# Low parts on one engine, regrouped block sums and a third weight buffer in a two-layer encoder kernel

## The chip, the cores and the metric

The kernel runs on one core of a Trainium2 chip. The metric is the device time of one execution in microseconds (us). A core has five engines that run their own instruction streams: TensorE (PE in the profile; its weight loads are PEld), VectorE (DVE), ScalarE (ACT), GpSimd (POOL) and SyncE (SP), which here only issues DMAs. An engine runs its instructions in the order in which they stand, and waits on semaphores for others. 128x512 means 128 partitions by 512 elements.

## The reference

Two encoder layers on 256 tokens of width 2048, in float32. Each layer has token-mixer heads and four heads that attend into 256 memory tokens, an output projection, and a squared-ReLU MLP of width 8192. The change sits almost wholly in the MLP:

```
n = rms_norm(h, mlp_norm[i])
h = h + jnp.square(jax.nn.relu(n @ w_up[i])) @ w_down[i]
...
return rms_norm(h, final_norm)
```

## The kernel before

**Three products for one.** TensorE multiplies a rounded float32 type. To keep precision, each operand is split into a high part (ACT copies it to the rounded type) and a low part (source minus high part, on DVE); each block product is then three matmuls, high by high, high by low and low by high. `split` writes both parts. So all weights, 398 MB read from memory, pass through ACT and one subtraction on the way to TensorE.

**The steps of the MLP.** After six leading up chunks, each layer runs 58 equal steps (`STEPS`, from the table `RUNS`). A step `n` has four grains, in this order: the first part of a down product, two halves of one up chunk (`ps_u`, 24 matmuls of 256 columns each), and the second part of the down product. The down products use Strassen's scheme in Winograd's form: a block of 2 by 2 sub-blocks of activations (`c`, from which `squared` makes seven left factors, split into `a_s`) times a block of 2 by 2 sub-blocks of weights takes seven products, `p1` to `p7`, of three 512-column matmuls each, instead of eight. The four sub-blocks of weights arrive as one tile `b` (`load` of `down_grains`); `pre` adds three or four sums of them, the tile `t`; `prep_first` splits `b` into `bh`, `bl`, and `prep_second` splits `t` into `th`, `tl`. The products accumulate in seven PSUM banks over a run of 4, 6 or 8 steps. At the end of a run `taken` adds each bank to a result column of `h` or to a sum `z` in SBUF, and after the last run of a column half `folded` adds the `z` to `h` in eight operations, spread over the following grains.

**Buffers.** The tiles `bh`, `bl`, `th`, `tl` have one buffer each: the split for step n+1 can begin only when step n's matmuls on that tile are over. The up halves `uh`, `ul` have two. `b`, `T` (holds `t`) and `U` (raw up chunks) have two each. How many grains ahead a load, `pre` and a split are placed is a triple per grain (`ahead`, `SOON`, `SOONER`).

**Who makes the low parts.** Inside the 58 steps the low part of the first up half is made on DVE, that of the second half on POOL (`half_of_side(..., engine=nc.gpsimd if hf and not lead else None)`); all other low parts are on DVE. POOL also issues one DMA a step that adds `b[:, 1]` into `b[:, 3]` in place (L1074); it waits for the sum at L1073, which still needs the old `b[:, 3]`, and `prep_first` waits for its landing.

After the steps the rest of the down weights runs as plain products (`plain_grains`), and in layer 1 `finish` normalises and stores the two token halves.

The order on each engine is set when the program is built, by the order in which these functions run and by a list scheduler on top.

Of the kernel before, what the change touches and what calls it, by code (L numbers as in the profile page):

```python
# [157 lines left out]
def encoder_kernel(ctx: ExitStack, tc: tile.TileContext, t: dict, out: bass.AP):  # L158
# [62 lines left out]
    soon = {}  # L221
    for c, src in ((FIRST_CHUNKS, t["w_km0"][3]), (FIRST_CHUNKS + 1, t["w_vm0"][0])):
        soon[c] = at.work.tile([P, CH], F32, tag="l4", name="raw_l4")
        nc.sync.dma_start(soon[c], src)
    ident = const.tile([P, P], F32, name="ident")
    ones = const.tile([P, P], F32, name="ones")
    nc.gpsimd.memset(ones, 1.0)
# [246 lines left out]
            plan.append(Work("M", blocks[b][0][c], acts, c * 4, begins, last, start, blocks[b][1]))  # L474


    def split(dst_hi, dst_lo, src, engine=None):

        first = nc.scalar.activation(dst_hi, src, AF.Copy)  # L479
        engine = engine or nc.vector  # L480
        return first, engine.tensor_tensor(dst_lo, src, dst_hi.bitcast(F32), op=ALU.subtract)  # L481

    def rstd_of(ss, n, name):

# [361 lines left out]
    def o_done(layer, nb):  # L846
# [16 lines left out]
        def scaled(b):  # L863

            if b < 2:
                box["room", b] = at.side.tile([P, 2, 1024], F32, tag="b", bufs=2, name="h_t")
# [71 lines left out]

    FIRST = ("p3", 6, 0), ("p1", 0, 1), ("p2", 2, 2), ("p5", 3, 3)
    SECOND = ("p7", 4, 0), ("p6", 5, 1), ("p4", 1, 2)

    def half_of_side(raw, hf, place=0, engine=None):
        s = slice(place // 4, place // 4 + HALF)
        tiles = tuple(at.side.tile([P, HALF + 64], F32R, tag=n, bufs=2, name=n)[:, s] for n in ("uh", "ul"))
        box.setdefault("splits", []).append(split(*tiles, raw[:, hf * HALF : (hf + 1) * HALF], engine))
        return tiles

    def loaded(src, tag):  # L950
        raw = at.side.tile([P, CH], F32, tag=tag, bufs=2, name=f"raw_{tag}")
        nc.sync.dma_start(raw, src)
        return raw

    def up_grains(layer, m):
        own = {}
        lead = m < LEAD

        def load():
            own["raw"] = loaded(t[f"w_up{layer}"][m], "U")  # L960

        def prep(hf):

            with tc.issue_after(box["summed"].ins) if m in (1, 2) else nullcontext():
                prepared(hf)

        def prepared(hf):
            half = 2 * m + hf
            if lead and (half in (2, 4) or half > 4 and half % 3 == 2):

                if half < 5:
                    room = at.side.tile([P, 2, HALF], F32R, tag="b", bufs=2, name="u_b")
                    own[hf] = room[:, 0], room[:, 1]
                else:
                    s = slice(U_AT // 4, U_AT // 4 + HALF)
                    own[hf] = tuple(at.mlp.tile([P, 3 * 512], F32R, tag=x, name=f"u_{x}")[:, s] for x in ("th", "tl"))
# [36 lines left out]
    def squared(layer, m, ps):  # L1013
# [12 lines left out]
            a = at.mlp.tile([P, 2, 4, P], F32R, tag="a", bufs=6, name="a_p")  # L1026
            split(a[:, 0], a[:, 1], c[:, :4])
        else:
            for d, x, y, op in ((4, 2, 0, ALU.subtract), (5, 1, 0, ALU.add), (6, 5, 2, ALU.subtract),
                                (7, 3, 6, ALU.subtract)):  # L1030
                box["made"] = nc.vector.tensor_tensor(c[:, d, :], c[:, x, :], c[:, y, :], op=op)  # L1031
# [22 lines left out]
    def down_grains(layer, n, begins, ends, sooner):  # L1054
# [12 lines left out]

        def pre():

            b, s = own["b"], at.side.tile([P, 3, 512], F32, tag="T", bufs=2, name="t")  # L1070

            with tc.issue_after(box["made"].ins) if n == 2 else nullcontext():
                box["t3"] = nc.vector.tensor_tensor(s[:, 0, :], b[:, 3, :], b[:, 0, :], op=ALU.add)  # L1073
            nc.gpsimd.dma_start(b[:, 3, :], b[:, 1, :], accum_op=ALU.add)  # L1074
            nc.vector.tensor_tensor(s[:, 1, :], s[:, 0, :], b[:, 1, :], op=ALU.add)
            nc.vector.tensor_tensor(s[:, 2, :], s[:, 1, :], b[:, 2, :], op=ALU.add)  # L1076
            own["t"] = s

        def prep_first():
            own["first"] = tuple(at.mlp.tile([P, CH], F32R, tag=x, name=x) for x in ("bh", "bl"))  # L1080
            b = own["b"].rearrange("p a b -> p (a b)")
            if sooner:

                with tc.issue_after(box["t3"].ins):
# [2 lines left out]
                split(*own["first"], b)  # L1087

        def prep_second():
            own["second"] = tuple(at.mlp.tile([P, 3 * 512], F32R, tag=x, name=x) for x in ("th", "tl"))  # L1090
            split(*own["second"], own["t"].rearrange("p a b -> p (a b)"))

        def run(which, products):
# [18 lines left out]
        def after_second():  # L1112
# [1 line left out]
            if ends:  # L1114
                box["z_set"].add(q)
            if ends and j == STEPPED[q] - 1:
                folded(q, 0.5 if n == len(STEPS) - 1 else 2)

        return [Grain(lambda: run("first", FIRST), lambda: after(FIRST), load, behind(pre), behind(prep_first, 4 if n else 1),
                      SOONER if sooner else SOON),  # L1120
                Grain(lambda: run("second", SECOND), after_second, None, None, behind(prep_second), SOONER)]

    def open_strassen(layer):

        closed(*[x for x in reversed(list(pools)) if x in ("ps_acc", "ps_att")])
        at.sums = opened("ps_sums", space=bass.MemoryType.PSUM)
        first = [x[0] for x in FIRST]
        second = ["up"] + [x[0] for x in SECOND]
# [34 lines left out]
    def folded(q, gap):  # L1163
# [8 lines left out]
            return lambda: add_scaled(columns_of(i, q, b), z, factor[:, i : i + 1])  # L1172

        for n, fn in enumerate((out(1, 0, z1, inv), add(z6, z6, z1, ALU.subtract), add(z7, z6, z7, ALU.subtract),
                                add(z6, z6, z5), out(1, 1, z6, inv), out(0, 0, z7, inv), add(z7, z7, z5),
                                out(0, 1, z7, ninv))):
            later(1 + int(gap * n), lambda fn=fn: past(fn, box["splits"][-2]))

# [124 lines left out]
    def finish(w, i, bank, begin, end):  # L1303
# [35 lines left out]
        nc.scalar.activation(p[1], p[1], AF.Copy, scale=r)  # L1339
        nc.vector.tensor_scalar(p[2], p[2], r, None, op0=ALU.mult)  # L1340
# [304 lines left out]
```

## Time and profile before

| | us |
|---|---|
| median of 3 runs (2029.22 to 2033.86) | 2031.28 |
| span of the profiled execution, first to last instruction | 2032.0 |
| PE busy in it | 1999.7 |
| DVE busy in it | 1793.5 |
| layer 0, steps 2 to 57 (from 482.26 to 1060.81 us) | 578.55 |
| layer 1, the same steps (from 1405.33 to 1983.80 us) | 578.47 |

The profile gives the span of the profiled execution and no time around it; the median of the unprofiled runs is 0.7 us under the span. Busy time of PE is modelled, since matmuls are pipelined: a new matmul starts while the one before it drains. So a duration of a single matmul (277 ns for 256 columns) is not its price; the distance from one start to the next is. The same holds on a smaller scale on DVE and ACT, where an instruction's record begins a little before that of the one ahead of it ends.

### The profile page before, as it was taken

To read this page: it belongs to the slowest core of one execution; us is meant where nothing else is said; L and a number is where in the kernel's file an instruction comes from. 1 tells how busy PE (TensorE), PEld (TensorE's weight loads), DVE (VectorE), ACT (ScalarE), POOL (GpSimd) and SP (SyncE) were. 2 spreads that over 40 slices of the span, in tenths; PEclk is the share of its full clock that TensorE was granted. 3 is DMA by queue.
4 is the path that set the end of the run, shared out by engine and by line. 5 is a ranking of instruction groups with operands and counts; after the bars stand their busy time and mean duration, and the time that the engine had idled before them with its cause. 6 is when DMAs were issued, how large, how long until landed. Compare 5 with 4: busy or idle time off the path is not lost.

```text
span 2032.0 us, 32807 instructions
## 1 busy us (share of the span) xinstructions
PE 1999.7 (98%) x12920; PEld 1813.0 (89%) x12920; DVE 1793.5 (88%) x2024; ACT 1270.8 (63%) x1735; POOL 541.2 (27%) x261
## 2 busy tenths in 40 slices
PE   9999999999999999999999999999999999999998
PEld 8999999899999898888888888899999898898987
DVE  6777767589999999999999769779999999999997
ACT  6655545567676666666656566567666666666654
POOL 0000000003333544444430010003444544444440
PEclk9999999999999999999999999999999999999999
DMA  7856665667777777677766765557777676776763
GB/s 286 312 199 200 209 203 196 248 188 228 236 230 232 217 230 224 219 231 224 222 203 225 244 213 182 203 171 234 234 232 232 224 239 213 220 240 215 232 197 135
DMA packets 105708, 448.02 MB, mean 220 GB/s; under 512 B 10961, under 2 KB 38609, under 8 KB 58065
## 3 DMA queue, kind: packets, MB, share of 16 engines
q1 hardware_dynamic: 88560, 414.99, 58.7%
q0 software_dynamic: 16704, 30.42, 8.7%
q8 instruction: 101, 1.65, 0.3%
q10 hardware_dynamic: 288, 0.52, 0.1%
q14 instruction: 55, 0.44, 0.1%
HBM read 398.17 MB, written 4.19 MB: 198 GB/s over the span
## 4 chain that ended last, share of the span: by engine, by line
PE 77%; DVE 12%; issue 4%; DMA 3%; POOL 3%; ACT 1%; DVEq 0%; SPq 0%; POOLq 0%; ACTq 0%
PE ps_u L384 24%; PE ps_s L384 10%; PE ps_m L361 8%; PE ps_m L365 8%; PE ps_m L364 8%; PE p L1105 6%; PE p L1102 6%; PE p L1104 6%; POOL ul L481 3%; DVE ul L481 2%; DMA b<-in_w_pair 2%; DVE tl L481 2%; DVE t L1076 2%; DVE c L1031 1%; DVE t L1073 1%
## 5 line engine op out<-in xcount | busy, mean ns | idle before, releaser
L384 PE MATMUL ps_u<-hT,uh 128*128 128x256 f32 x3812 | 668.3, 277 | 0.0
L384 PEld LDWEIGHTS ps_u<-hT,uh 128*128 128x128 f32 x3812 | 581.9, 189 | 5.5
L384 PE MATMUL ps_u<-hT,ul 128*128 128x256 f32 x1960 | 545.7, 278 | 20.6 <-POOL ul L481 17.8
L481 POOL TENSOR_TENSOR ul<-raw_U,uh 128x1024 fp32r<-128x1024 f32 x116 | 417.3, 3597 | 261.1 <-ACT uh L479 261.1
L479 ACT ACTIVATE uh<-raw_U 128x1024 fp32r<-128x1024 f32 x262 | 276.2, 1058 | 231.2 <-PE ps_u L384 221.2
L384 PEld LDWEIGHTS ps_u<-hT,ul 128*128 128x128 f32 x1960 | 369.4, 188 | 24.7 <-POOL ul L481 19.8
L481 DVE TENSOR_TENSOR lo<-raw,hi 128x1024 fp32r<-128x1024 f32 (+1 forms) x215 | 254.7, 1191 | 98.4 <-ACT hi L479 97.3
L479 ACT ACTIVATE hi<-raw 128x1024 fp32r<-128x1024 f32 (+1 forms) x215 | 221.2, 1036 | 162.6 <-PE ps_m L365 84.7
L479 ACT ACTIVATE bh<-b 128x2048 fp32r<-128x2048 f32 x116 | 222.1, 1915 | 78.8 <-PE p L1105 76.3
L481 DVE TENSOR_TENSOR bl<-b,bh 128x2048 fp32r<-128x2048 f32 x116 | 265.0, 2284 | 1.0 <-ACT bh L479 1.0
L481 DVE TENSOR_TENSOR tl<-t,th 128x1536 fp32r<-128x1536 f32 x116 | 238.2, 2054 | 18.0 <-ACT th L479 17.8
L1074 POOL DMA_DIRECT2D b<-b x116 | 102.1, 880 | 525.1 <-DVE t L1073 361.4
L481 DVE TENSOR_TENSOR ul<-raw_U,uh 128x1024 fp32r<-128x1024 f32 x146 | 215.4, 1476 | 6.6 <-ACT uh L479 6.6
L479 ACT ACTIVATE th<-t 128x1536 fp32r<-128x1536 f32 x116 | 172.8, 1489 | 32.4 <-PE p L1105 30.5
L1104 PE MATMUL p<-bl,a_s 128*128 128x512 f32 x464 | 180.8, 390 | 1.6 <-DVE bl L481 1.6
L1105 PE MATMUL p<-bh,a_s 128*128 128x512 f32 x464 | 181.3, 391 | 0.0
L1102 PE MATMUL p<-bh,a_s 128*128 128x512 f32 x464 | 180.6, 389 | 0.0
L384 PE MATMUL ps_s<-nT,hi 128*128 128x256 f32 x896 | 154.7, 276 | 0.0
L1031 DVE TENSOR_TENSOR c<-c 128x128 f32<-128x128 f32 x240 | 144.6, 622 | 5.2 <-ACT c L1021 3.4
L1102 PE MATMUL p<-th,a_s 128*128 128x512 f32 x348 | 136.1, 391 | 0.0
L1104 PE MATMUL p<-tl,a_s 128*128 128x512 f32 x348 | 135.9, 391 | 0.0
L384 PEld LDWEIGHTS ps_s<-nT,hi 128*128 128x128 f32 x896 | 135.5, 188 | 0.2
(295 smaller groups left out, 3772.3 us busy)
## 6 DMA issues: line engine op xcount, KB each, us to landing
raw_U<-in_w_up SPq DMA_DIRECT2D x128, 1024.0 KB, 4.8
b<-in_w_pair SPq DMA_DIRECT2D x116, 1024.0 KB, 4.8
raw<-in_w_o SPq DMA_DIRECT2D x32, 1024.0 KB, 5.0
b<-b POOLq DMA_DIRECT2D x116, 256.0 KB, 3.3
raw<-in_w_b SPq DMA_DIRECT2D x21, 1024.0 KB, 5.1
raw<-in_w_av SPq DMA_DIRECT2D x12, 1024.0 KB, 4.9
raw<-in_w_aq SPq DMA_DIRECT2D x12, 1024.0 KB, 4.8
raw<-in_w_ak SPq DMA_DIRECT2D x12, 1024.0 KB, 4.7
```

The costliest lines, as they stand in the source:

```text
L361: first = nc.tensor.matmul(ps, ah, hi[:, s], start=st, stop=False)
L364: nc.tensor.matmul(ps, ah, lo[:, s], start=False, stop=False)
L365: final = nc.tensor.matmul(ps, al, hi[:, s], start=False, stop=sp)
L384: ins = nc.tensor.matmul(ps, x, acts[:, k, part], start=k == n == 0, stop=k == KT - 1 and n == 2)
L479: first = nc.scalar.activation(dst_hi, src, AF.Copy)
L481: return first, engine.tensor_tensor(dst_lo, src, dst_hi.bitcast(F32), op=ALU.subtract)
L1031: box["made"] = nc.vector.tensor_tensor(c[:, d, :], c[:, x, :], c[:, y, :], op=op)
L1074: nc.gpsimd.dma_start(b[:, 3, :], b[:, 1, :], accum_op=ALU.add)
L1076: nc.vector.tensor_tensor(s[:, 2, :], s[:, 1, :], b[:, 2, :], op=ALU.add)
L1102: ins = nc.tensor.matmul(ps, a[:, 0, ai, :], hi[:, s], start=begins, stop=False)
L1104: nc.tensor.matmul(ps, a[:, 0, ai, :], lo[:, s], start=False, stop=False)
L1105: nc.tensor.matmul(ps, a[:, 1, ai, :], hi[:, s], start=False, stop=ends)
```

## The change

All low parts go to DVE: `split` and `half_of_side` lose their engine argument. The four sums of `squared` become three operations, the second of which makes two blocks at once (with a sign turned, so that `folded` subtracts where it added). The block `b[:, 3] + b[:, 1]` is no longer made in place: ACT copies `b[:, 3]` into a fourth block of `t`, and the DMA adds `b[:, 1]` there, beside the three sums. So `bh`, `bl` shrink from 2048 to 1536 columns and `th`, `tl` grow from 1536 to 2048, and the product `p5` moves from a step's first part to its second. `b` gets a third buffer; the descriptor scratch of DMAs issued by POOL shrinks to 4096 bytes, which makes room for it; the loads of the down blocks are placed 12 grains ahead instead of 8. The fold after the first column half is spread at three grains instead of two. Outside the MLP, one early weight chunk is loaded in two DMAs, and `finish` stores each token half in three DMAs instead of four.

```diff
-        nc.sync.dma_start(soon[c], src)
+        for s in [slice(0, HALF), slice(HALF, CH)] if c == FIRST_CHUNKS else [slice(0, CH)]:
+            nc.sync.dma_start(soon[c][:, s], src[:, s])
...
-    def split(dst_hi, dst_lo, src, engine=None):
+    def split(dst_hi, dst_lo, src):
         first = nc.scalar.activation(dst_hi, src, AF.Copy)
-        engine = engine or nc.vector
-        return first, engine.tensor_tensor(dst_lo, src, dst_hi.bitcast(F32), op=ALU.subtract)
+        return first, nc.vector.tensor_tensor(dst_lo, src, dst_hi.bitcast(F32), op=ALU.subtract)
...
-    FIRST = ("p3", 6, 0), ("p1", 0, 1), ("p2", 2, 2), ("p5", 3, 3)
-    SECOND = ("p7", 4, 0), ("p6", 5, 1), ("p4", 1, 2)
+    FIRST = ("p3", 6, 0), ("p1", 0, 1), ("p2", 2, 2)
+    SECOND = ("p7", 4, 0), ("p6", 5, 1), ("p4", 1, 2), ("p5", 3, 3)
+    BANKS = ("p3", "p1", "p2", "p5"), ("up", "p7", "p6", "p4")
...
-                own[hf] = half_of_side(own["raw"], hf, engine=nc.gpsimd if hf and not lead else None)
+                own[hf] = half_of_side(own["raw"], hf)
...
-            for d, x, y, op in ((4, 2, 0, ALU.subtract), (5, 1, 0, ALU.add), (6, 5, 2, ALU.subtract),
-                                (7, 3, 6, ALU.subtract)):
-                box["made"] = nc.vector.tensor_tensor(c[:, d, :], c[:, x, :], c[:, y, :], op=op)
+            nc.vector.tensor_tensor(c[:, 4, :], c[:, 0, :], c[:, 2, :], op=ALU.subtract)
+            nc.vector.tensor_tensor(c[:, 5:7, :], c[:, 0:5:4, :], c[:, 1, None, :].to_broadcast([P, 2, P]), op=ALU.add)
+            box["made"] = nc.vector.tensor_tensor(c[:, 7, :], c[:, 3, :], c[:, 6, :], op=ALU.subtract)
...
-            own["b"] = at.side.tile([P, 4, 512], F32, tag="b", bufs=2, name="b")
+            own["b"] = at.side.tile([P, 4, 512], F32, tag="b", bufs=3, name="b")
...
-            b, s = own["b"], at.side.tile([P, 3, 512], F32, tag="T", bufs=2, name="t")
+            b, s = own["b"], at.side.tile([P, 4, 512], F32, tag="T", bufs=2, name="t")
+            nc.scalar.activation(s[:, 3, :], b[:, 3, :], AF.Copy)
+            nc.gpsimd.dma_start(s[:, 3, :], b[:, 1, :], accum_op=ALU.add)
...
-            nc.gpsimd.dma_start(b[:, 3, :], b[:, 1, :], accum_op=ALU.add)
...
-                folded(q, 0.5 if n == len(STEPS) - 1 else 2)
+                folded(q, 0.5 if n == len(STEPS) - 1 else 3)
...
-                      SOONER if sooner else SOON),
+                      (12, 8, 4) if sooner else (12, 5, 4)),
...
-        p = [h[:, i, a:b] for a, b in ((0, 256), (256, 768), (768, x))]
+        p = [h[:, i, a:b] for a, b in ((0, 512), (512, x))]
...
-        for eng, a, b in ((nc.sync, 0, 256), (nc.sync, x, D), (nc.scalar, 256, 768), (nc.sync, 768, x)):
+        for eng, a, b in ((nc.sync, x, D), (nc.scalar, 0, 512), (nc.sync, 512, x)):
...
-    nc = _bacc.Bacc("TRN2", target_bir_lowering=False, num_devices=1)
+    nc = _bacc.Bacc("TRN2", target_bir_lowering=False, num_devices=1, dynamic_dma_scratch_size=4096)
```

**DVE in an ordinary step.** Below is what stands on DVE in one step of layer 0 before (a step in which a pair of up chunks is done, so that the split `a_s` and three of the four sums `c` are in it; the fourth stands one step earlier); `t<-b` and `t<-t,b` are the sums of `pre`.

```order
L1073 TENSOR_TENSOR t<-b 128x512
L1075 TENSOR_TENSOR t<-t,b 128x512
L481 TENSOR_TENSOR bl<-b,bh 128x2048
L1076 TENSOR_TENSOR t<-t,b 128x512
L481 TENSOR_TENSOR ul<-raw_U,uh 128x1024
L1031 TENSOR_TENSOR c<-c 128x128 x3
L481 TENSOR_TENSOR tl<-t,th 128x1536
L481 TENSOR_TENSOR a_s<-c,a_s 128x896
```

The same place of the changed program, where all lines behind the first edit stand one further down:

```order
L481 TENSOR_TENSOR bl<-b,bh 128x1536
L1076 TENSOR_TENSOR t<-b 128x512
L481 TENSOR_TENSOR ul<-raw_U,uh 128x1024
L1077 TENSOR_TENSOR t<-t,b 128x512
L481 TENSOR_TENSOR ul<-raw_U,uh 128x1024
L1078 TENSOR_TENSOR t<-t,b 128x512
L1030 TENSOR_TENSOR c<-c 128x128
L1031 TENSOR_TENSOR c<-c 128x256
L1032 TENSOR_TENSOR c<-c 128x128
L481 TENSOR_TENSOR tl<-t,th 128x2048
L481 TENSOR_TENSOR a_s<-c,a_s 128x896
```

DVE has a second `ul` per step, three operations for the sums `c`, and the 512 columns of the added block have moved from `bl` to `tl`. POOL's stream in the MLP, which held an `ul` and a DMA per step, now holds 58 DMAs in a row per layer.

**ACT in an ordinary step.** Before, a step without a pair (`u` is the small copy of an up chunk's first columns, with its buffer's number in the name):

```order
L479 ACTIVATE th<-t 128x1536
L479 ACTIVATE bh<-b 128x2048
L984 ACTIVATE u_5817<-raw_U 128x128
L479 ACTIVATE uh<-raw_U 128x1024 x2
L1020 ACTIVATE c<-ps_u 128x256
L1021 ACTIVATE c<-c 128x256
```

After, the same:

```order
L480 ACTIVATE th<-t 128x2048
L480 ACTIVATE bh<-b 128x1536
L985 ACTIVATE u_6025<-raw_U 128x128
L1072 ACTIVATE t<-b 128x512
L480 ACTIVATE uh<-raw_U 128x1024 x2
L1021 ACTIVATE c<-ps_u 128x256
L1022 ACTIVATE c<-c 128x256
```

The copy that the DMA adds to stands between the split of `b` and those of the up halves, one step ahead of the `th` that reads its result.

**DVE behind the end of the run that `folded` follows** (layer 0, just behind step 51; the `z` are the sums in SBUF, `first` is the tile that holds `h`). Before:

```order
L481 TENSOR_TENSOR tl<-t,th 128x1536
L1169 TENSOR_TENSOR z_4605<-z_4605 128x512
L1031 TENSOR_TENSOR c<-c 128x128
L1073 TENSOR_TENSOR t<-b 128x512
L481 TENSOR_TENSOR bl<-b,bh 128x2048
L481 TENSOR_TENSOR ul<-raw_U,uh 128x1024
```

After:

```order
L481 TENSOR_TENSOR tl<-t,th 128x2048
L1170 TENSOR_TENSOR z_4606<-z_4606 128x512
L1031 TENSOR_TENSOR c<-c 128x256
L481 TENSOR_TENSOR ul<-raw_U,uh 128x1024
L1076 TENSOR_TENSOR t<-b 128x512
L481 TENSOR_TENSOR bl<-b,bh 128x1536
```

Here an `ul` now stands ahead of the `bl` that the next step's first product waits for; before it stood behind it.

More of the change, by code (lines that the diff above doesn't have):

```diff
@@ L865, in scaled @@
             if b < 2:
-                box["room", b] = at.side.tile([P, 2, 1024], F32, tag="b", bufs=2, name="h_t")
+                box["room", b] = at.side.tile([P, 2, 1024], F32, tag="b", bufs=3, name="h_t")
                 y = box["room", b][:, 0]
@@ L932, in add_o, with half_of_side @@
                 plan[-1].behind = plan[-2].behind = plan[-1].last_block = True
-    FIRST = ("p3", 6, 0), ("p1", 0, 1), ("p2", 2, 2), ("p5", 3, 3)
-    SECOND = ("p7", 4, 0), ("p6", 5, 1), ("p4", 1, 2)
-    def half_of_side(raw, hf, place=0, engine=None):
+    FIRST = ("p3", 6, 0), ("p1", 0, 1), ("p2", 2, 2)
+    SECOND = ("p7", 4, 0), ("p6", 5, 1), ("p4", 1, 2), ("p5", 3, 3)
+    BANKS = ("p3", "p1", "p2", "p5"), ("up", "p7", "p6", "p4")
+    def half_of_side(raw, hf, place=0):
         s = slice(place // 4, place // 4 + HALF)
         tiles = tuple(at.side.tile([P, HALF + 64], F32R, tag=n, bufs=2, name=n)[:, s] for n in ("uh", "ul"))
-        box.setdefault("splits", []).append(split(*tiles, raw[:, hf * HALF : (hf + 1) * HALF], engine))
+        box.setdefault("splits", []).append(split(*tiles, raw[:, hf * HALF : (hf + 1) * HALF]))
         return tiles
     def loaded(src, tag):
-        raw = at.side.tile([P, CH], F32, tag=tag, bufs=2, name=f"raw_{tag}")
+        raw = at.side.tile([P, CH], F32, tag=tag, bufs=2 + (tag == "b"), name=f"raw_{tag}")
         nc.sync.dma_start(raw, src)
@@ L971, in prepared @@
                 if half < 5:
-                    room = at.side.tile([P, 2, HALF], F32R, tag="b", bufs=2, name="u_b")
+                    room = at.side.tile([P, 2, HALF], F32R, tag="b", bufs=3, name="u_b")
                     own[hf] = room[:, 0], room[:, 1]
@@ L975, in prepared @@
                     s = slice(U_AT // 4, U_AT // 4 + HALF)
-                    own[hf] = tuple(at.mlp.tile([P, 3 * 512], F32R, tag=x, name=f"u_{x}")[:, s] for x in ("th", "tl"))
+                    own[hf] = tuple(at.mlp.tile([P, CH], F32R, tag=x, name=f"u_{x}")[:, s] for x in ("th", "tl"))
                 box["splits"].append(split(*own[hf], own["raw"][:, hf * HALF : (hf + 1) * HALF]))
             else:
-                own[hf] = half_of_side(own["raw"], hf, engine=nc.gpsimd if hf and not lead else None)
+                own[hf] = half_of_side(own["raw"], hf)
             if not lead and hf == 0:
@@ L1079, in prep_first @@
         def prep_first():
-            own["first"] = tuple(at.mlp.tile([P, CH], F32R, tag=x, name=x) for x in ("bh", "bl"))
-            b = own["b"].rearrange("p a b -> p (a b)")
+            own["first"] = tuple(at.mlp.tile([P, 3 * 512], F32R, tag=x, name=x) for x in ("bh", "bl"))
+            b = own["b"][:, :3].rearrange("p a b -> p (a b)")
             if sooner:
@@ L1089, in prep_second @@
         def prep_second():
-            own["second"] = tuple(at.mlp.tile([P, 3 * 512], F32R, tag=x, name=x) for x in ("th", "tl"))
+            own["second"] = tuple(at.mlp.tile([P, CH], F32R, tag=x, name=x) for x in ("th", "tl"))
             split(*own["second"], own["t"].rearrange("p a b -> p (a b)"))
@@ L1126, in open_strassen @@
         at.sums = opened("ps_sums", space=bass.MemoryType.PSUM)
-        first = [x[0] for x in FIRST]
-        second = ["up"] + [x[0] for x in SECOND]
+        first, second = BANKS
         box["ps"], box["unused"] = {}, set()
```

5 lines of the change are left out of this document (2 added, 3 removed).

## The prediction

> **What bounds the kernel now.** I read the page's busy times first, then who waited for whom on PE, then the chain of waits in order of time, then the time line of the places where PE waited.
>
> ```profile
> span 2032.0 us, 32807 instructions
> ...
> PE 1999.7 (98%) x12920; PEld 1813.0 (89%) x12920; DVE 1793.5 (88%) x2024; ACT 1270.8 (63%) x1735; POOL 541.2 (27%) x261
> ```
>
> PE is busy for 98% of the span, so no change that leaves the matmuls alone can win more than about 32 us. This one leaves them alone: the same seven products of three matmuls, one of them moved. The question is only which part of PE's lost time goes. PE's own waits:
>
> ```profile
> PE ps_u L384 <- POOL ul L481: 17.8, 10, 3.3
> PE ps_u L384 <- DVE ul L481: 2.6, 5, 0.9
> PE p L1104 <- DVE bl L481: 1.6, 2, 1.0
> ```
>
> (us in total, times, longest.) Nearly all of it is for the low part of the second up half, made on POOL: ten waits, 17.8 us. What such a wait costs in the end is read from the chain, where each step's 48 up matmuls are a piece, when they ran without a break:
>
> ```profile
> 482.26 5.45 PE ps_u L384 x48
> 492.49 5.45 PE ps_u L384 x48
> ...
> 1060.81 5.45 PE ps_u L384 x48
> ...
> 1405.33 5.45 PE ps_u L384 x48
> ...
> 1983.80 5.45 PE ps_u L384 x48
> ```
>
> A step without a wait takes 492.49 - 482.26 = 10.23 us. From step 2 to step 57 are 55 steps: 55 x 10.23 = 562.6 us, against 578.55 in layer 0 and 578.47 in layer 1. So the steps lose 16.0 + 15.9 = **31.9 us**, more than the waits name, since weight loads and the pipe behind a wait start anew. Now why POOL is late:
>
> ```profile
> 1009.59 2.28 DVE L481 TENSOR_TENSOR bl<-b,bh 128x2048 fp32r<-128x2048 f32 x1
> 1009.97 0.88 POOL L1074 DMA_DIRECT2D b<-b  x1 [6.78 <-DVE t L1073]
> ...
> 1011.36 9.53 POOL L481 TENSOR_TENSOR ul<-raw_U,uh 128x1024 fp32r<-128x1024 f32 x1 [0.51 <-ACT uh L479]
> ...
> 1011.79 1.22 DVE L481 TENSOR_TENSOR ul<-raw_U,uh 128x1024 fp32r<-128x1024 f32 x1
> ```
>
> The POOL subtraction takes 9.53 us while DVE works beside it without a gap. Over the layers and in layer 0's steps (ns, min/median/max):
>
> ```profile
> L481 DVE TENSOR_TENSOR ul<-raw_U,uh x146: 1186/1220/3455, 369.8 to 2008.9; 128x1024 fp32r<-128x1024 f32 x146
> L481 POOL TENSOR_TENSOR ul<-raw_U,uh x116: 2394/3284/9540, 458.4 to 1980.1; 128x1024 fp32r<-128x1024 f32 x116
> L481 DVE TENSOR_TENSOR tl<-t,th x57: 1740/1752/3455, 459.7 to 1051.0; 128x1536 fp32r<-128x1536 f32 x57
> L1031 DVE TENSOR_TENSOR c<-c x112: 276/286/2504, 457.9 to 1031.5; 128x128 f32<-128x128 f32 x112
> L481 DVE TENSOR_TENSOR a_s<-c,a_s x28: 1079/1085/1090, 464.4 to 1035.1; 128x896 fp32r<-128x896 f32 x28
> L481 DVE TENSOR_TENSOR bl<-b,bh x57: 2277/2284/2292, 466.1 to 1052.7; 128x2048 fp32r<-128x2048 f32 x57
> L1073 DVE TENSOR_TENSOR t<-b x56: 674/687/2742, 463.1 to 1043.1; 128x512 f32<-128x512 f32 x56
> L1075 DVE TENSOR_TENSOR t<-t,b x56: 677/687/694, 463.8 to 1045.9; 128x512 f32<-128x512 f32 x56
> L1074 POOL DMA_DIRECT2D b<-b x56: 880/880/887, 464.1 to 1044.1; - x56
> L1076 DVE TENSOR_TENSOR t<-t,b x56: 676/685/2910, 465.4 to 1047.6; 128x512 f32<-128x512 f32 x56
> ```
>
> The two engines shut each other out. POOL's subtraction is 2.4 us at best and four times that at worst; DVE operations have a firm floor (their medians) and, in some executions, two microseconds more: those are the ones that met a running POOL subtraction. `bl` and L1075, which stand where POOL is issuing its DMA or idle, are never late, and the DMA is 880 to 887 ns although `bl` runs beside it. So the subtraction costs both engines, the DMA issue neither.
>
> **The change, part by part.**
>
> *Low parts to DVE.* It removes 116 POOL subtractions and adds 116 of 1.22 us on DVE. The cover for this is that DVE's stretched operations fall back to their medians. A step on DVE then, by medians: two `ul` 2 x 1.22; `tl`, now 2048 columns, 2.28 (row `bl`); `bl`, now 1536, 1.75 (row `tl`); three sums `t` 3 x 0.69; half a pair's `a_s` 0.54; half a pair's sums `c`. These become three operations, two of 0.29 and one of 256 columns, which no row here shows; it lies between 0.29 (128) and 0.69 (512), and I take 0.42, a third of the way by columns. Half a pair: 0.50. Sum 9.57 us of a step of 10.23. The records overlap, though:
>
> ```profile
> 1050.44 0.68 DVE L481 TENSOR_TENSOR a_p<-c,a_p 128x512 fp32r<-128x512 f32 x1
> 1051.05 1.75 DVE L481 TENSOR_TENSOR tl<-t,th 128x1536 fp32r<-128x1536 f32 x1
> 1052.71 2.28 DVE L481 TENSOR_TENSOR bl<-b,bh 128x2048 fp32r<-128x2048 f32 x1
> 1054.92 1.21 DVE L481 TENSOR_TENSOR ul<-raw_U,uh 128x1024 fp32r<-128x1024 f32 x1
> ```
>
> From start to start these take 0.61, 1.66 and 2.21 us, 0.08 less than their durations. With nine operations a step that makes 9.57 - 0.72 = **8.85 us of 10.23**: 1.4 us free in a step.
>
> [...]
>
> *Does each part come in time?* A step's clock: 69 matmuls; the 48 of up take 5.45 us, so the 21 others 0.228 each. Let F, the first part (now 9 matmuls), start at 0: F ends at 2.05, the up halves at 4.8 and 7.5, S, the second part (now 12), at 10.23. ACT's prices:
>
> ```profile
> L479 ACT ACTIVATE uh<-raw_U 128x1024 fp32r<-128x1024 f32 x115 | 121.3, 1059 | 105.3 <-PE ps_u L384 105.2
> L479 ACT ACTIVATE bh<-b 128x2048 fp32r<-128x2048 f32 x57 | 109.2, 1915 | 38.3 <-PE p L1105 38.3
> L479 ACT ACTIVATE th<-t 128x1536 fp32r<-128x1536 f32 x57 | 84.9, 1489 | 15.7 <-PE p L1105 15.7
> ```
>
> `th` (1.9, as `bh` was) can start at 0, when the S before is over; DVE's `tl` runs 1.9 to 4.2, and S needs it at 7.5: 3.3 us to spare. `bh` 2.05 to 3.6, `bl` to 5.9, with an `a_s` between to 6.9; the next F needs it at 10.23: 3.3 to spare. `ul` of the first half ends near 8, needed at 12.3; of the second (ready at 8.6) near 9.7, needed at 15. At a run's end `taken` adds six operations on 128x512, about 0.7 each by row L1075: 4 us within a step, against 1.4 free in it and 1.4 in the next. Those of the three F products fall where DVE waits for `th` anyway; the rest makes the next `tl` some 1 us late, `bl` about the same. The spare 3.3 us covers it, and all banks are read long before the next step writes them. Behind the run that `folded` follows, eight more operations (5.5 us) come over six steps, 0.9 a step of the 1.4. There the order has an `ul` ahead of `bl`; worked through row by row, `bl` ends some 0.1 us after F asks for it. I put 0.5 us per layer there, **1.0 us** in all. ACT was busy for 63% of the span; the rows above lie on a line (0.43 us per 512 columns), by which the new 512-column copy is some 0.6 us, 6% of a step.
>
> *Three-operation sums.* They are in the sum above; DVE's free time hides them, and without them a step would have 0.1 us less.
>
> *The added block.* `bl` no longer waits for the DMA; `th` now does. ACT copies at about 4.6, the DMA is issued at 5.2, and `th` wants it at 10.23, on pain of a stall from 13.5 on (7.5 of the next step, less 1.9 and 2.3). Landings of DMAs on `b`, the loads included:
>
> ```profile
> DMA to landing us min/median/max: 3.3/4.7/7.9
> ```
>
> 5.2 + 7.9 = 13.1 is in time. Behind `th` on ACT stand `bh` and the `uh` of that step, which share the 3.3 us. Cost 0. Its other end: nothing is won either, since PE never waited for this DMA.
>
> *Third buffer, loads 12 grains ahead, 4 KB of scratch.* PE waits for no load in the list above, so the earlier loads win 0 on PE by themselves; they keep ACT's copy from standing in front of a late load. The smaller scratch could hold up an issue: at the low end 0, at the high end each issue waits until the DMA before has landed. That one was issued 10.23 us earlier and landed after 7.9 at most, so both ends are 0.
>
> *The ends.* The last stores: the final half's ScalarE part loses 256 columns and DVE's gains them; the last DMA leaves some 0.1 us earlier and is 256 columns larger. I take 0, with 0.5 us on either side. The split early load touches nothing that PE waits for: 0.
>
> **The sum**, against the profiled execution: 2032.0 - 31.9 + 1.0 = 2001.1 us. The median of the runs is 0.7 us below the profiled span, so I predict **2000.4 us**, 1.5% less.
>
> **The rivals.**
>
> *DVE becomes the bound in bursts.* If durations count in full, a step has 0.65 us free and not 1.4, and a run's end and the fold (24 + 24 + 8 operations of 0.7, 39 us a layer) use it up: 58 x 9.57 + 39 = 594 us against 58 x 10.23 = 593, plus 0.6 to 1.4 us in each of some steps in which DVE stands waiting for `th`. That is 1 to 7 us per layer: 2002 to 2015 us; I say 2009. The starts above speak against it, the tight `bl` behind the fold for it. [...]
>
> *DVE does not get faster, and the change costs.* If the stretched operations owe their two microseconds to something else than POOL's subtractions (POOL's DMA, or loads into the same memory), they stay stretched. In layer 0 a step would then have at least the 9.57 us, and the means of before on top: each `ul`, `tl`, `c` and L1073, L1076 about 0.2 to 0.35 longer, 1.8 us in all. 8.85 + 1.8 + 0.6 for run ends and folds = 11.3 us: 1.0 us over PE's step, 116 times. 2000 + 120 = **2120 us**. It decides from 10.5 us of DVE work per step on, where the 31.9 us are used up. Against it: the DMA's 880 to 887 ns and the firm 2277 to 2292 of `bl` beside it.
>
> *The DMA-added block comes late.* Every step loses what the landing takes beyond 8.3 us. With 9 us at each of 116 steps, 80 us; with a few at 10 us, 5 to 10 us, about 2008 us. The 7.9 us maximum speaks against it.
>
> *PE's lost time is not the waits'.* If the stalls only move, from `ul` to `tl` at the same places (run ends), half of them stays: 2016 us.
>
> **How the numbers follow.** Forecast 0.70 (1997 to 2005); DVE bursts 0.14 (2009); late block 0.05 (2008); stalls that move 0.06 (2016, at worst 2032); DVE not faster 0.05 (2120). The range of 8 in 10 takes the forecast's own spread, its low end with no stall left (1999.4) and 2 us of scatter as the runs before show, and reaches over most of the bursts: **1997 to 2012**. Under 0.2% (4 us) a measurement of this kernel can't be told from no change. Slower by that: 0.05, from the second rival; within it: 0.03, from stalls that move; faster: 0.92.
>
> **What would show it.** Right: POOL's group `ul` is gone, DVE's maxima fall to their medians (`t<-b` 2.7 to 0.7 us, `c` 2.5 to 0.3), the time from step 2 to 57 falls from 578.5 to about 563 us per layer, and PE's list of waits has nothing in it over 1 us but near the fold. Wrong: DVE over 98% of those stretches, waits of PE for `bl` or `tl`; ACT `th` waiting for a DMA; POOL's DMA longer than 0.9 us.

## The result, and the profile after

The changed kernel takes **2002.72 us** (median of 4 runs, 2002.14 to 2003.76) against 2030.25 of the kernel before in runs beside it (4 runs, 2028.27 to 2033.86): ratio **0.986**, 95% interval 0.9841 to 0.9878. The forecast was 2000.4, its range 1997 to 2012. The profiled execution took 2002.73 us by its own time, and its span, against which the prediction's sum was made, is 2001.0; the sum said 2001.1.

The page after, busy time per engine in us, share of the span, and instructions:

```profile
span 2001.0 us, 32691 instructions
...
PE 1989.8 (99%) x12920; PEld 1806.7 (90%) x12920; DVE 1718.8 (86%) x2080; ACT 1329.9 (66%) x1849; POOL 123.0 (6%) x145
```

DVE has 116 subtractions more to do and is busy for 75 us less: the stretched operations of before alone lasted some 206 us longer than the others of their kind, 114 of them by 1.8 us each. Who PE waits for after (us in total, times, longest):

```profile
PE ps_m L362 <- DVE z L1157: 2.0, 2, 1.0
PE idle L236 <- POOL mhalf L230: 1.0, 1, 1.0
PE ps_m L362 <- ACT cat L480: 0.5, 1, 0.5
```

The three waits shown of before (22.0 us) are gone, and the first line is new. The chain after, in order of time (start, us, what), at steps 2 and 3, around the fold, at step 57, and at steps 2 and 57 of layer 1:

```profile
479.79 5.45 PE ps_u L385 x48
490.02 5.45 PE ps_u L385 x48
...
991.12 5.45 PE ps_u L385 x48
1001.66 5.66 PE ps_u L385 x48
1012.11 5.45 PE ps_u L385 x48
...
1042.79 5.45 PE ps_u L385 x48
...
1388.38 5.45 PE ps_u L385 x48
...
1951.38 5.45 PE ps_u L385 x48
```

Step 2 to step 57 takes 563.0 us in both layers (before 578.55 and 578.47); 55 steps of 10.23 are 562.6. What is left is at one place: from 991.12 to 1012.11 are two steps and 20.99 us, 0.5 too many, behind the fold. The same rows give the whole account of the 31.0 us of span. Up to step 2: 482.26 - 479.79 = 2.5 won. Steps of layer 0: 15.55 won. From there to step 2 of layer 1: 344.52 before, 345.59 after, 1.1 lost. Steps of layer 1: 15.5 won. From there to the end: 48.2 before, 49.6 after, 1.4 lost.

DVE's and POOL's groups after (duration in ns, minimum/median/maximum):

```profile
L481 DVE TENSOR_TENSOR ul<-raw_U,uh x262: 1181/1218/1243, 368.4 to 1978.3; 128x1024 fp32r<-128x1024 f32 x131
L481 DVE TENSOR_TENSOR tl<-t,th x116: 2277/2293/2294, 458.8 to 1952.1; 128x2048 fp32r<-128x2048 f32 x116
L1031 DVE TENSOR_TENSOR c<-c x60: 410/424/427, 438.9 to 1923.5; 128x256 f32<-128x256 f32 x60
L1076 DVE TENSOR_TENSOR t<-b x116: 677/684/689, 437.5 to 1934.9; 128x512 f32<-128x512 f32 x116
L1073 POOL DMA_DIRECT2D t<-b x116: 862/872/1051, 437.1 to 1935.4; - x116
```

Maxima lie on the medians: `ul` 3455 to 1243, `t<-b` 2742 to 689, while POOL still issues a DMA in every step. The one operation that no row of before showed, `c` with 256 columns, takes 0.42 us, the value chosen between 0.29 and 0.69. DVE's free time can be read as well: in steps 14 to 17 of layer 0 it stands still for 0.9 and 1.4 us in turn, 1.15 in the mean; the prediction had 1.4.

The new wait is where the steps end and the plain products begin. The time line there (start, us, engine, line, operation, and in brackets the idle time and who ended it):

```profile
1051.31 0.74 DVE L1146 SCALAR_TENSOR_TENSOR first<-p,inv,first 128x512 f32<-128x512 f32 x1
1051.97 0.68 DVE L481 TENSOR_TENSOR a_p<-c,a_p 128x512 fp32r<-128x512 f32 x1
1052.57 0.68 DVE L1157 TENSOR_TENSOR z<-p,z 128x512 f32<-128x512 f32 x1
...
1053.31 0.50 PE L362 MATMUL ps_m<-uh,a_s 128*128 128x512 f32 x1 [0.98 <-DVE z L1157]
```

One of PE's first plain products (its third group of three matmuls) needs a PSUM bank (`ps_m`) that the last Strassen product, now `p5`, still holds until DVE has added it to its `z`, the last of four such operations. PE's matmul before started at 1051.94; instead of 0.23 us later the next starts 1.37 later: 1.14 us, and as much in layer 1.

### The profile page after: what moved, and what is told of

Its sections match the earlier page's. It is cut to its first block, busy times and chain, and to the rows that moved or that the text cites. A ratio compares the mean times of both kernels' runs of the same rounds, so it can differ in the third digit from the quotient of the medians.

```text
span 2001.0 us, 32691 instructions
## 1 busy us (share of the span) xinstructions
PE 1989.8 (99%) x12920; PEld 1806.7 (90%) x12920; DVE 1718.8 (86%) x2080; ACT 1329.9 (66%) x1849; POOL 123.0 (6%) x145
## 4 chain that ended last, share of the span: by engine, by line
PE 98%; DVE 1%; issue 0%; DMA 0%; ACT 0%; SPq 0%; DVEq 0%; POOLq 0%; POOL 0%; ACTq 0%
PE ps_u L385 35%; PE ps_s L385 10%; PE p L1106 9%; PE p L1104 9%; PE p L1107 9%; PE ps_m L362 8%; PE ps_m L365 8%; PE ps_m L366 8%; PE sc_ps L538 0%; PE av L612 0%; PE sc_ps L539 0%; PE sc_ps L537 0%; PE av L611 0%; PE av L613 0%; DMA raw<-in_w_first 0%
## 5 line engine op out<-in xcount | busy, mean ns | idle before, releaser
L481 DVE TENSOR_TENSOR ul<-raw_U,uh 128x1024 fp32r<-128x1024 f32 x262 | 318.4, 1219 | 15.6 <-ACT uh L480 15.4
L481 DVE TENSOR_TENSOR tl<-t,th 128x2048 fp32r<-128x2048 f32 x116 | 265.6, 2290 | 71.4 <-ACT th L480 71.0
L480 ACT ACTIVATE th<-t 128x2048 fp32r<-128x2048 f32 x116 | 222.7, 1920 | 117.4 <-PE p L1107 114.8
L481 DVE TENSOR_TENSOR bl<-b,bh 128x1536 fp32r<-128x1536 f32 x116 | 203.2, 1752 | 0.0
L1104 PE MATMUL p<-th,a_s 128*128 128x512 f32 x464 | 181.2, 391 | 0.0
L1107 PE MATMUL p<-th,a_s 128*128 128x512 f32 x464 | 180.5, 389 | 0.0
L480 ACT ACTIVATE bh<-b 128x1536 fp32r<-128x1536 f32 x116 | 172.4, 1486 | 7.9
L1073 POOL DMA_DIRECT2D t<-b x116 | 101.0, 871 | 1143.9 <-ACT t L1072 1060.7
L1107 PE MATMUL p<-bh,a_s 128*128 128x512 f32 x348 | 136.2, 391 | 0.0
L1106 PE MATMUL p<-bl,a_s 128*128 128x512 f32 x348 | 135.7, 390 | 0.0
L1104 PE MATMUL p<-bh,a_s 128*128 128x512 f32 x348 | 135.4, 389 | 0.0
L385 PE MATMUL ps_s<-nT,lo 128*128 128x256 f32 x448 | 123.7, 276 | 0.0
```

The lines of the kernel that those rows point to most:

```text
L385: ins = nc.tensor.matmul(ps, x, acts[:, k, part], start=k == n == 0, stop=k == KT - 1 and n == 2)
L481: return first, nc.vector.tensor_tensor(dst_lo, src, dst_hi.bitcast(F32), op=ALU.subtract)
L1073: nc.gpsimd.dma_start(s[:, 3, :], b[:, 1, :], accum_op=ALU.add)
L1104: ins = nc.tensor.matmul(ps, a[:, 0, ai, :], hi[:, s], start=begins, stop=False)
L1106: nc.tensor.matmul(ps, a[:, 0, ai, :], lo[:, s], start=False, stop=False)
L1107: nc.tensor.matmul(ps, a[:, 1, ai, :], hi[:, s], start=False, stop=ends)
```

## The experiments

Each kernel was timed against the kernel before on its own chip, whose median there was between 2031.6 and 2032.6 us.

**1. POOL's low part back into the changed kernel.** All other edits stay.

```diff
-                own[hf] = half_of_side(own["raw"], hf)
+                own[hf] = half_of_side(own["raw"], hf, engine=nc.gpsimd if hf and not lead else None)
```

> The changed kernel, with the low part of the second up half back on POOL and all else as changed. Theory A (POOL's subtraction and DVE's operations with two SBUF inputs shut each other out, and that alone lost the steps' 32 us): POOL's ul is 2.4 us at best and 7 us or more at worst again, DVE's tl, c and t reach 2 us over their medians, PE waits for POOL ul, and the steps lose 15 to 35 us: 2015 to 2035 us, although DVE has 1.1 us a step less to do. Theory B (DVE's amount of work was the bound, and the other edits relieved it): DVE has even more free time, so PE waits for nothing new and the time is 2003 us or less.

Measured: 2034.21 us (2032.11 to 2036.3, 10 runs), ratio 1.0014 (1.0005 to 1.0023). The whole gain is gone. Groups, and who PE waits for:

```profile
L481 DVE TENSOR_TENSOR ul<-raw_U,uh x146: 1171/1219/3456, 368.4 to 2010.9; 128x1024 fp32r<-128x1024 f32 x146
L481 POOL TENSOR_TENSOR ul<-raw_U,uh x116: 2389/2942/6808, 455.2 to 1980.4; 128x1024 fp32r<-128x1024 f32 x116
```

```profile
PE ps_u L385 <- DVE ul L481: 14.6, 13, 1.6
PE p L1106 <- DVE tl L481: 6.3, 5, 2.2
...
PE ps_u L385 <- POOL ul L481: 0.5, 2, 0.3
```

DVE has less to do than in the changed kernel and is late all the same. PE now waits for DVE and hardly for POOL, where theory A had expected the wait for POOL. So in this kernel it isn't that POOL is too slow for its share: its subtraction holds DVE up (`ul` on DVE 3.46 us at worst against 1.22 in the median, 13 waits of PE for it).

**2. The low parts alone, in the kernel before.**

```diff
-                own[hf] = half_of_side(own["raw"], hf, engine=nc.gpsimd if hf and not lead else None)
+                own[hf] = half_of_side(own["raw"], hf)
```

> The kernel before, with only one edit: the low part of the second up half on DVE. Theory A: DVE's maxima fall to their medians, a step is about 8.95 us of DVE work from start to start, and nearly all of the gain is there: 2001 to 2006 us. Theory B (the added work fits only because of the three-operation sums, the moved block and the third buffer): DVE is too full, PE waits for bl and tl, 2010 us or more. Rival C (the accumulating DMA in front of bh matters once POOL is free): PE waits for bl at L1104, 1 us or more at several steps.

Measured: 2001.22 us (2000.96 to 2001.48, 4 runs), ratio 0.9851 (0.9834 to 0.9867). This one edit has the whole gain; with all the others the time is 1.5 us longer.

**3. `p5` at the head of the second part.** In the changed kernel:

```diff
-    SECOND = ("p7", 4, 0), ("p6", 5, 1), ("p4", 1, 2), ("p5", 3, 3)
+    SECOND = ("p5", 3, 3), ("p7", 4, 0), ("p6", 5, 1), ("p4", 1, 2)
```

> The changed kernel with p5 as the first product of a step's second part instead of the last. In the changed kernel PE waits 1.0 us (1.14 us lost) in each layer at the second token half of the first plain block, until DVE has added the p5 bank to z, the last of four such operations. Theory: it is p5's bank that the plain block takes over, so with p5 first this wait goes and 2.3 us of the span with it, to 1998 to 1999.5 us of span. Rival: the block waits for whichever operation of the four is last (then p4's), and the wait stays at 1 us; time as the changed kernel, 2002 to 2003 us.

Measured: 1999.91 us (1999.70 to 1999.97, 4 runs), ratio 0.9844 (0.9829 to 0.9859). PE's waits are then:

```profile
PE idle L236 <- POOL mhalf L230: 1.0, 1, 1.0
PE ps_m L362 <- ACT cat L480: 0.5, 1, 0.5
PE ps_s L385 <- ACT hi L480: 0.3, 1, 0.3
```

The wait for `z` is gone, and with it 2.8 us; it was the moved product's bank. The traces show it in place: from step 57 of layer 0 to step 2 of layer 1 this kernel takes 344.29 us (1042.78 to 1387.07) and the changed one 345.59, and from step 57 of layer 1 to the end 48.3 and 49.6, which makes 2.6 of the 2.8 us. Run again on another chip than this one, the changed kernel as it is gave 2002.77 (2002.34 to 2002.99), so a difference between chips isn't likely to be the cause:

> The changed kernel as it is, on the same chip as the two others, to hold the small differences against: 2002 to 2004 us. Were it at 2000 us, the 2.9 us that moving p5 to the front of the second part brought would be a difference between chips.

**4. The block added in place again.** In the changed kernel, with `p5` in the first part, no ACT copy, and the two column counts as before:

```diff
-            nc.scalar.activation(s[:, 3, :], b[:, 3, :], AF.Copy)
-            nc.gpsimd.dma_start(s[:, 3, :], b[:, 1, :], accum_op=ALU.add)
...
+            nc.gpsimd.dma_start(b[:, 3, :], b[:, 1, :], accum_op=ALU.add)
```

> The changed kernel with the added block in place again (the DMA adds into the fourth block of b, which bh and bl read; p5 in the first part; no copy on ACT). Theory A: PE never waited for this block, so within 2 us of the changed kernel; the 1.1 us wait at the plain blocks goes, since p5's bank is read earlier, so 2000 to 2003 us. Rival C: bh now waits for the DMA (5.2 us to landing in the changed kernel), bl comes late and PE waits at L1104's products in many steps: 2005 us or more.

Measured: 1999.33 us (1998.73 to 2001.95, 4 runs), ratio 0.9844 (0.9829 to 0.9858). The DMA-added block beside the sums wins nothing; with it came the move of `p5`, whose wait is the loss. This and the third kernel are the best two that were run, and can't be told apart.

**5. Which POOL operation holds DVE?** The kernel of experiment 2, with one more POOL operation of 128x1024 floats for each of the 116 steps, on a scratch tile `pl` that nobody else uses (the DMA scratch is 4 KB to make room):

```diff
+                if hf and not lead:
+                    nc.gpsimd.memset(box["pl"], 1.0)
```

in the first kernel; `nc.gpsimd.tensor_tensor(pl, pl, pl, op=ALU.subtract)` in the second; `nc.gpsimd.tensor_scalar(pl, pl, 1.0, None, op0=ALU.mult)` in the third.

> The kernel of before with every low part on VectorE (2001.2 us), plus one POOL memset of 128x1024 floats in each of the 116 steps, into a scratch tile that nobody reads; the DMA scratch is 4 KB to make room for it. [...] Theory W (any POOL operation on SBUF shuts DVE out): DVE stretched about 100 times as in before, 2050 to 2130 us.

> The same, with a POOL subtraction of 128x1024 floats (scratch minus scratch, into scratch) in place of the memset; nobody waits for its result. [...] Theory P (what cost before its time was that PE waited for POOL's slow result, not that DVE was held): nobody waits for this one, 2001 to 2004 us.

> The same, with a POOL multiplication of the scratch tile by a constant (one input in SBUF). [...]

Measured: 2000.22 (2000.03 to 2001.39), 2162.91 (2162.34 to 2163.64) and 2046.42 us (2045.54 to 2048.0), 4 runs each. Groups of POOL's operation and of DVE's `ul`, `memset` first:

```profile
L481 DVE TENSOR_TENSOR ul<-raw_U,uh x262: 1183/1218/1226, 368.5 to 1975.0; 128x1024 fp32r<-128x1024 f32 x131
...
L981 POOL MEMSET pl<- x116: 952/957/1322, 419.8 to 1395.0; 128x1024 f32 x116
```

Then the subtraction, then the multiplication:

```profile
L481 DVE TENSOR_TENSOR ul<-raw_U,uh x262: 1176/1219/2912, 369.1 to 2137.5; 128x1024 fp32r<-128x1024 f32 x131
...
L981 POOL TENSOR_TENSOR pl<-pl x116: 1893/2754/11221, 420.3 to 1648.0; 128x1024 f32<-128x1024 f32 x116
```

```profile
L481 DVE TENSOR_TENSOR ul<-raw_U,uh x262: 1171/1218/2057, 368.7 to 2020.5; 128x1024 fp32r<-128x1024 f32 x131
...
L981 POOL TENSOR_SCALAR pl<-pl x116: 2770/3542/4406, 419.9 to 1615.3; 128x1024 f32<-128x1024 f32 x116
```

A POOL operation that only writes leaves DVE alone: 108 of DVE's `TENSOR_TENSOR` with both inputs in SBUF overlap a memset, and none is longer by 0.1 us. One that reads SBUF holds it, with one input or two, though its result is for nobody: beside the subtraction 108 of DVE's `TENSOR_TENSOR` are longer by over 0.1 us, by 1.7 in the mean, beside the multiplication 110, by 0.8. DVE's busy time over the span goes the same way, with the same work on it: 1727.3, 1914.4 and 1809.8 us. Theories W and P fall; what stands is the first half of theory A in experiment 1, and a POOL operation with one input is enough for it. One thing was not as planned: with nothing to wait for, the scheduler put the extra operations early, the memsets in one row of some 67 us per layer, the subtractions mostly three or four to a step in the first twelve steps, the multiplications two or three in the first twenty-one, and ten or more of each ahead of the first step (the rows' last starts, 1395, 1648 and 1615 us, show that they end early). So 2163 us isn't the price of one in each step.

**6. How much of DVE was free?** The same subtraction on DVE: in the kernel of experiment 2; in that of experiment 3, with two buffers for `b`; and in that of experiment 4.

```diff
+                if hf and not lead:
+                    nc.vector.tensor_tensor(box["pl"], box["pl"], box["pl"], op=ALU.subtract)
```

> The kernel of before with every low part on VectorE, plus one more DVE subtraction of 128x1024 floats (1.22 us) in each of the 116 steps, on a scratch tile that nobody reads. This measures how much of DVE's time was free. If a step is what DVE's starts say (8.85 + 1.22 = 10.07 of 10.23 us), it fits, and only the fold and the run ends wait: 2002 to 2015 us. If the durations count in full (9.57 + 1.22 = 10.79 us), DVE sets the step: 116 x 0.56 = 65 us more, 2066 us, and PE waits for DVE in nearly every step.

> The changed kernel with p5 first in the second part, two buffers for down blocks in place of three, and the same extra DVE subtraction (1.22 us a step, unread scratch) as in m4_dve_more, where it cost 78 us. There DVE's starts were idle for up to 3.8 us at a time behind the ACT copy of b, which waited for the DMA-added block, which waits for a DVE sum. Theory C (chain: the in-place block ties DVE, DMA, ACT and DVE into one ring, and DVE had room): with the block added beside, the ring is open, and 8.85 + 1.22 = 10.07 us fit into 10.23: 2000 to 2012 us. Theory F (DVE is full: durations count, 9.57 + 1.22 = 10.79 us): 116 x 0.56 = 65 us above 1999.9, 2055 to 2080 us, wherever the block is added.

> The changed kernel with the block added in place (as in e4_in_place, 1999.3 us), three buffers for down blocks, and the same extra DVE subtraction. Theory C: the ring is there as in m4_dve_more, and a third buffer only lets the next load start earlier: 2050 to 2080 us. Theory B (it was the second buffer that came free late): 2000 to 2012 us. Theory F: 2055 to 2080 us.

Measured: 2079.6 (2077.03 to 2082.1), 2071.97 (2070.24 to 2073.4) and 2083.87 us (2081.6 to 2084.92). The three are alike and far from the times that theories C and B named for a kernel with room. But here too the operations ran ahead, ten or eleven before the first step and mostly two or three to a step in the next seventeen to twenty-one. So the runs don't answer the question as it was put, and C, B and F are all left open. In the second of these kernels the operation was then tied to its step, by reading the high part of its own half:

```diff
-                    nc.vector.tensor_tensor(box["pl"], box["pl"], box["pl"], op=ALU.subtract)
+                    nc.vector.tensor_tensor(box["pl"], box["pl"], own[hf][0].bitcast(F32), op=ALU.subtract)
```

> The same as n1_dve_more_beside, but the extra DVE subtraction (1.22 us, 1.14 from its start to the next) reads the high part of its own block half, so that it can't run ahead of its step: in n1, n2 and m4 the extra operations came in the first half of each layer only, about two to a step, and so those runs did not measure one more in each step. Theory S (starts count: 8.85 + 1.14 = 9.99 of 10.23 us, so one fits into every step): 2000 to 2015 us, waits only at the fold and at run ends. Theory F (durations count: 9.57 + 1.22 = 10.79): 2055 to 2080 us, a wait in nearly every step. In n1 118 x 1.14 = 135 us of DVE's time cost 73 us of steps, so 62 us of idle time were found in some 52 steps, 1.2 us a step; that speaks for S, and for 116 x 1.2 = 139 us of room against 116 x 1.14 = 132 needed.

Measured: 2080.05 us (2079.14 to 2081.94). F has nearly the time and not the way there, S the way in ordinary steps and not the time. The chain:

```profile
599.93 5.45 PE ps_u L385 x48
610.16 5.45 PE ps_u L385 x48
...
651.07 5.45 PE ps_u L385 x48
661.29 5.45 PE ps_u L385 x48
...
725.09 5.45 PE ps_u L385 x48
735.32 5.45 PE ps_u L385 x48
752.18 6.41 PE ps_u L385 x48
```

From 599.93 to 661.29 are six steps of 10.23: the extra operation fits into an ordinary step, as S says, and as it couldn't if durations counted (10.79 us); in each of these steps DVE still stands idle for 0.2 to 0.5 us. From 735.32 to 752.18 is one step and 6.6 us more, just ahead of the last step of a run. In layer 0, 41 of the 57 distances from one step to the next are 10.23; ten others, in pairs at five of the run ends, lose 36 us. What is late there is the seven factors of a pair:

```profile
PE p L1108 <- ACT a_s L480: 25.6, 9, 2.8
PE p L1111 <- DVE a_s L481: 13.5, 9, 2.4
```

They aren't late for want of time on DVE, which stood idle for 0.51 us just before (745.48). On ACT (first the tied kernel, then the same pair in that of experiment 3):

```profile
743.53 1.91 ACT L480 ACTIVATE th<-t 128x2048 fp32r<-128x2048 f32 x1 [1.06 <-PE p L1111]
745.35 0.94 ACT L480 ACTIVATE a_s<-c 128x896 fp32r<-128x896 f32 x1
```

```profile
725.25 0.93 ACT L480 ACTIVATE a_s<-c 128x896 fp32r<-128x896 f32 x1
```

In the kernel of experiment 3 the factors are made at the end of step 25, some 8 us ahead of their use in step 27; in the tied kernel at the end of step 26, behind a `th` that waits for PE. In layer 0 it is the same at all five places (steps 9, 25, 33, 41 and 49 there, 10, 26, 34, 42 and 50 here). So by these rows what costs most of the 80 us is the order that was built around the added operation, and not DVE's room; no kernel with the same operation and another order was run.

## Why the prediction was right, and where not

*The cause* was right: POOL's reading subtraction and DVE's two-input operations shut each other out (2034.21 us with it in experiment 1, 2001.22 without it in experiment 2; a memset in its place leaves 2000.22 in experiment 5). In the trace of before, the 116 POOL subtractions overlap some 370 DVE `TENSOR_TENSOR`, but only 112 of these are stretched, about one for each and by 1.8 us in the mean. So the prediction's word that `L1075`, never late, stands where POOL issues its DMA or is idle isn't right: in layer 0 it overlaps a POOL subtraction 16 times in 56. How the two take turns, and why POOL's operation takes 9.53 us at worst against 2.39 at best, no view shows. Where DVE's inputs lie makes a difference in one view of before: with one input in PSUM (`p`) nothing is stretched, 692 ns at most; with both in SBUF (`z`, `first`) one of three is, 2895 ns.

```profile
L1156 DVE TENSOR_TENSOR z<-p,z x20: 674/678/692, 656.1 to 1004.9; 128x512 f32<-128x512 f32 x20
...
L1145 DVE SCALAR_TENSOR_TENSOR first<-z,inv,first x3: 742/746/2895, 1000.8 to 1025.4; 128x512 f32<-128x512 f32 x3
```

Of DVE's operations with an input in PSUM, 29 overlap a POOL subtraction by over 0.1 us in before, and none takes over 0.76 us. A DVE operation with one input alone never ran beside one, so whether it would be held isn't shown.

*Steps* were right: forecast 31.9 us won and 1.0 left; measured 15.55 + 15.47 = 31.0, with 0.5 left per layer at the predicted place. The reason given for it holds too: the first matmul on `bl` there starts 0.40 us after the one before it and not 0.23 (999.14 to 999.54), released by DVE's `bl`, and the next one 0.11 late. The other 0.2 are a slow up half, which the last section shows.

*"Since weight loads and the pipe behind a wait start anew"* was at most a part of the reason why the steps lost more than their waits name. In the windows of before (length, then busy time of PE, PEld, DVE, ACT and POOL, the granted clock, DMA share, GB/s) behind the longest wait, and in the chain there:

```profile
1021.75:1025.10 3.35, 3.35 (x18) 3.35 (x17) 3.35 (x3) 0.00 (x0) 0.87 (x1) 0.51 0.97 303
```

```profile
1020.95 4.39 PE ps_u L384 x22
```

PE ran at half its clock for 3.4 us: 22 matmuls took 4.39 us and not 2.50 (22 x 5.45/48). This came once a layer, and it makes about 3 of the 10 us by which the steps lost more than the 15 waits in them name. About 4 are a slow new start, an estimate from this one wait (15 x 0.27): from the last matmul ahead of this wait to the first behind it are 3.55 us (1017.40 to 1020.95), which is 0.16 more than the 3.27 that the wait names and the usual 0.11; the next comes after 0.22 instead of 0.11. Where the other 3 us lie isn't shown. That weight loads have a part in it isn't shown. The sum didn't depend on this reason, since it was read from the steps.

*Three-operation sums, third buffer, loads, scratch*, put at 0, are small, but perhaps not nothing. The kernel of experiment 4 has them, with the later fold and the edits at the two ends; that of experiment 2 has none of them, and on the same chip is 1.9 us slower by the medians (one of the four runs of experiment 4 isn't faster). From step 2 to step 57 the former takes 562.5 us in both layers, the latter 562.9 and 563.6, so some 1.5 of the 1.9 us are lost behind the fold. Which edit does it, or whether one pays for another, wasn't tried singly.

*"All banks are read long before the next step writes them"* failed. It looked at the steps alone; behind the last step PE doesn't wait a step before it asks for a bank. The move of `p5` costs 2 x 1.1 us there by the trace and 2.8 us by experiment 3. It isn't seen in the span because some 2.5 us were won ahead of step 2: 1.2 of them in the first 28 us of the run, which the change leaves nearly alone and where single executions differ (the kernel of experiment 2, with the start of before, is 0.9 us ahead of before there as well), and 1.1 in steps 0 and 1, which the sum left out. So it is luck that the sum, 2001.1, meets the span of 2001.0 to 0.1 us.

*"The median of the runs is 0.7 us below the profiled span"* was the mis-sized term of the sum. In all runs of both kernels the time is 1.7 to 1.9 us over the span of the same execution. The 0.7 came from a profiled execution that was the slowest of the three; that scatter (2028 to 2034) belongs to the waits and goes with them (after, 2002.1 to 2003.8). With 2001.1 + 1.8 = 2002.9, the sum comes to 0.2 us of the median, by the same luck.

*The rivals.* DVE as the bound in bursts didn't come. How far off it is isn't shown: with 1.14 us more in each step ordinary steps still keep their time, and what five of a layer's run ends lose, 7 us each, is the order's doing by the rows of experiment 6. Durations counted in full, the condition of this rival, don't give the right room: the tied kernel's ordinary steps ran in 10.23 us and not in 10.79. DVE that stays stretched, a late block and stalls that move weren't seen. Landings of the added block did grow, from 3.3 to 5.2 us by the page's median:

```profile
b<-in_w_pair SPq DMA_DIRECT2D x116, 1024.0 KB, 5.7
...
t<-b POOLq DMA_DIRECT2D x116, 256.0 KB, 5.2
```

but nobody waited for them. Why they grew wasn't tried.

## What to carry to other kernels

Work given to POOL wasn't free here, where it reads SBUF while VectorE has two inputs there: one subtraction a step on POOL makes 2034.2 us, on DVE 2002.7 (experiment 1). Look for a DVE group whose maximum is far over its median, and take the share back even if DVE's sum of work grows. Count room on an engine from start to start: by starts a step of experiment 6 had 9.99 us of DVE's work, by durations 10.79, and ordinary steps kept their 10.23. When an operation is added, look also at what the order built around it puts later: in experiment 6 the operation fitted in, and seven factors came a step too late. When a product or a copy is moved within a loop, look also at who asks for its bank behind the loop's last turn: here it was 1.14 us a layer.

## What was not expected of the hardware

In some places a wait of PE cost more than its length. In the tied kernel, PE stood for 2.84 and 1.71 us close together near 746 us; the windows before and behind it:

```profile
702.00:742.00 40.00, 40.00 (x274) 36.81 (x273) 39.55 (x41) 28.24 (x33) 3.48 (x4) 1.00 0.69 214
...
749.40:753.70 4.30, 4.30 (x16) 3.70 (x15) 3.69 (x6) 1.48 (x2) 0.20 (x1) 0.50 0.36 61
```

For 4.3 us the granted clock is 0.50, and a 128x512 matmul starts 0.43 us after the one before it instead of 0.23. In before it was 0.51 over the 3.35 us shown above, behind the wait of 3.3 us. In the kernel of experiment 1, where PE's longest wait was 2.2 us, PE is busy for 1.24 of 3.40 us at a granted clock of 1.00, and then it is 0.50:

```profile
1006.00:1009.40 3.40, 1.24 (x10) 0.92 (x9) 3.40 (x5) 0.00 (x0) 0.00 (x0) 1.00 0.18 77
1009.80:1012.80 3.00, 3.00 (x8) 2.32 (x7) 3.00 (x4) 2.95 (x6) 1.52 (x2) 0.50 0.37 64
```

In before, twelve waits with 1.0 to 2.0 us from start to start left the clock alone, and the two of 3.55 halved it, which cost 1.9 us more each (4.39 us for 22 matmuls instead of 2.50). In the kernel with POOL's multiplication PE waits 32 times for `bl`, up to 2.6 us, and the mean granted clock is 0.997. What decides whether the clock is halved isn't shown.

Apart from that, behind the 0.2 us wait at the fold the up half at 1001.66 takes 5.66 us instead of 5.45, at a granted clock of 1.00 in that window; what makes these 4% stays open. In layer 1 the same half takes 5.66 us too (1910.25).
